# One scheduling block, ordered by a finer model, around the whole body of a two-block transformer kernel

## The chip, the cores and the metric

The kernel runs on one core of a Trainium2 chip. TensorE (PE) multiplies matrices, VectorE (DVE), ScalarE (ACT) and GpSimd (POOL) do the rest, and SyncE (SP) issues the DMA transfers. The metric is the time of one execution in microseconds (us). Each engine, and the queue on SP, works through its instructions in the order that the program gives it; the engines wait for each other on semaphores.

## The reference

Two transformer blocks follow each other on one sequence of 512 tokens of width 1024, all in fp32. The first has two layers that are modulated by a condition vector:

```python
cond = jax.nn.silu(c)
for layer in range(DEPTH):                       # DEPTH = 2
    mod = cond @ w_ada[layer] + b_ada[layer]     # 1024 -> 3 x 1024
    shift, scale, gate = jnp.split(mod, 3, axis=-1)
    h = rmsnorm(x, g_pre[layer]) * (1.0 + scale[:, None, :]) + shift[:, None, :]
    if layer % 2 == 0: y = even_mixer(h, ...)
    else:              y = odd_mixer(h, ...)
    x = x + gate[:, None, :] * rmsnorm(y, g_post[layer])
```

The even mixer has 8 heads of latent attention (MLA: low-rank queries, keys and values, plus a rotary part) and 8 heads of attention over a sliding window of 128 with sinks. The odd mixer has 4 heads of differential attention and 8 heads of forgetting attention. Each is gated by `silu` and multiplied by an output weight. The second block has one mixer with three parts: 6 heads of sparse attention (compressed, selected and windowed keys), 4 heads of stick-breaking attention, and 6 heads of HGRN, a gated recurrence worked out in chunks of 64 tokens; then the output weight, a scaled residual and a layer norm.

## The kernel before, in words

All tensors are held with the width or the tokens on the 128 partitions. The products keep fp32 accuracy by splitting each operand into a high and a low part (`hh`, `hl` of the activations; `whi`, `wlo` of the weights): one product is three matmuls (`mm3`, whose matmuls have line L79). A weight piece of 128 x 1024 comes by DMA into `wraw` (L106), ACT casts it to `whi` (L108) and DVE forms the residue `wlo` (L112); this loader has a raised priority (`WP`).

The stages run in this order: setup and the first h (0 to 60 us in the profile), projection and rotary steps (to 115), the sliding-window heads (to 211), the MLA setup (to 250) and MLA heads (to 309), the output product with the first residual (to 345), the odd mixer (to 610), the second residual (to 646), and the second block: projections and the HGRN scan (to about 803), stick-breaking (to 869), sparse attention (to 991), and the output product with the layer norm.

The modulation is worked out in the background. `gemv_steps` yields one step at a time: `wada` loads a 128 x 1024 piece of `w_ada` into the tile `graw` (L156), and `gemv_acc` adds it, times an element of `cond`, to the accumulator `sa` on DVE (L174 for the first of eight pieces, L176 for the others). `graw` has one buffer, so a piece can be loaded only when the product before it is done. Heads call `hook`, which takes steps of this background product and, by a credit, weight chunks from the queue `fq`, so that PE has filling beside the softmax work. In the program's names `sa_435` is the accumulator of the first layer's gate, and `sa_777` that of the second layer's gate.

The residual (L601 to L614) forms row statistics, adds the gated output to x, and then `hgen` (L238, L240) normalises each block of rows, which PE transposes into the new `hh` and `hl`. In the MLA setup the keys and queries of a pair of heads are split into four tiles (`qk_425` to `qk_428`, L326) and copied to other partitions by DMA (L366). In the HGRN scan the score products are `sr <- sa, tmpr`.

No order is written out by hand: the Tile framework's scheduler takes the instructions in the order in which the code makes them, with the priorities above, and decides how they stand on each engine and on SP's queue. The rotating buffers (PSUM: `acc` 3, `s` 2, `t` 2, `o` 1; SBUF: `wraw` 2, `whi` 4, `graw` 1 and others) are fixed in the tables at the head of the class `Kern`. The change touches the first line of `build`, which makes the whole body.

Of the kernel before, what the change touches and what calls it, by code (L numbers as in the profile page):

```python
# [1716 lines left out]


def build(tc, I, O, stage=3):
    with ExitStack() as ctx:  # L1720
        K = Kern(ctx, tc, I, O)
        nc = K.nc
        K.setup()
        K.modv = {}

        def done0(part, acc):
            K.mod_done(part, acc)

        def steps0():
            yield from K.gemv_steps(1, (0, 1), K.mod_done)  # L1730
            yield from K.gemv_steps(0, (2,), lambda part, acc: K.gate_sum(0, acc))

        K.back = steps0()
        og = K.even()
        K.bg(100)
        put = lambda b, xb: nc.sync.dma_start(O["out"][b * 128:(b + 1) * 128, :], xb)
        if stage == 1:
            K.residual(I["w_out0"], [2, 3, 0, 1], og, put)
            return
        a1 = K.mod_a(1, K.modv[1])  # L1740
        nc.vector.tensor_scalar(a1, a1, -0.5, None, ALU.mult)
        rows = K.spread(a1), K.spread(K.modv[0])
        K.new_h()
        xd = K.dram([4, 128, D])

        def nxt(b, xb):
            nc.sync.dma_start(xd[b], xb)
            return K.hgen(b, xb, rows)

        K.residual(I["w_out0"], [2, 3, 0, 1], og, nxt)  # L1750
        K.xd = [xd[b] for b in range(4)]
        K.back = K.gemv_steps(1, (2,), lambda part, acc: K.gate_sum(1, acc))
        og = K.odd()
        K.bg(100)
        if stage == 2:
            K.residual(I["w_out1"], [0, 1, 2, 3], og, put)
            return
        K.new_h()
        xd2 = K.dram([4, 128, D])

        def nxt2(b, xb):
            nc.sync.dma_start(xd2[b], xb)
            return K.hgen(b, xb)

        K.residual(I["w_out1"], [0, 1, 2, 3], og, nxt2)
        K.xd = [xd2[b] for b in range(4)]
        tr = K.load("cst_2", [128, 512], "cst")
        K.strict = tr[:, 256:384]
        K.ones2 = tr[:, 384:512]
        K.tri = K.t([128, 128], "tri", 1, F32R)  # L1770
        K.mones = K.t([128, 128], "mones", 1, F32R)
        nc.vector.tensor_copy(K.tri, tr[:, 0:128])
        nc.vector.tensor_copy(K.mones, tr[:, 128:256])
        og = K.second()
        K.tail(I["w_out2"], K.TO, og)
# [148 lines left out]
```

## Time and profile before

| | |
|---|---|
| median of 3 runs | 1039.86 us (1039.27 to 1048.97) |
| profiled execution | 1036.68 us, span 1035.0 us |
| mean granted TensorE clock | 0.974 of full speed |
| PE, DVE, ACT, POOL busy | 934.3, 709.4, 535.8, 246.2 us |
| DMA queue, share of 16 engines | 44.9% |

The span runs from the first to the last instruction of the profiled execution; its own time is 1.7 us longer. Busy time counts the time in which an engine has an instruction in work, so that idle time is the span less that. In the rows of the profile buffer numbers are left out of the names, and `L79` is line 79 of the kernel. A timeline row gives the start, the length, the engine, the line, the operation, output and inputs, and in brackets the idle time before and what ended it.

### The profile page before, as it was taken

What the parts mean: (1) busy time and instruction counts of PE and PEld (TensorE: products, weight loads), DVE (VectorE), ACT (ScalarE), POOL (GpSimd) and SP (SyncE); (2) the same over time, 40 slices, a digit from 0 to 9 for tenths busy, and PEclk for the clock granted to TensorE, in tenths of its full rate; (3) what the DMA queues carried; (4) which work ended last, traced back from release to release, by engine and by line L of the source; (5) the groups of instructions that cost most, each with busy time, mean ns of one, the idle gap of its engine ahead of it and who ended that gap; (6) DMA issues with size and microseconds to landing.
All of it is one profiled execution on the core that took longest, in us unless ns stands there. A gap on an engine that the chain in (4) does not pass through costs nothing.

```text
span 1035.0 us, 14792 instructions
## 1 busy us (share of the span) xinstructions
PE 934.3 (90%) x4999; PEld 766.3 (74%) x4999; DVE 709.4 (69%) x1581; ACT 535.8 (52%) x1181; POOL 246.2 (24%) x274
## 2 busy tenths in 40 slices
PE   3989996878998899999999999999977989999896
PEld 2767875766776887788887778987866768777675
DVE  5876665866877866875366666466689486577757
ACT  6433653836754434475355843454533484565820
POOL 1220122201430002221011420043145133444440
PEclk9899998889999999999999999999999999999998
DMA  9656544365556366661564343343401623331242
GB/s 359 221 170 200 147 100 134 90 148 137 168 169 199 121 209 166 158 168 42 164 152 117 133 138 121 100 123 107 138 21 52 170 51 97 103 95 38 64 140 82
DMA packets 56672, 137.38 MB, mean 133 GB/s; under 512 B 15048, under 2 KB 15432, under 8 KB 56597
## 3 DMA queue, kind: packets, MB, share of 16 engines
q1 hardware_dynamic: 56596, 136.44, 44.9%
q8 instruction: 40, 0.66, 0.3%
q14 instruction: 36, 0.29, 0.1%
HBM read 105.42 MB, written 8.44 MB: 110 GB/s over the span
## 4 chain that ended last, share of the span: by engine, by line
PE 39%; DVE 9%; ACT 4%; issue 2%; POOL 2%; DMA 1%; SPq 0%; DVEq 0%; POOLq 0%; ACTq 0%
PE accr L79 28%; PE sr L79 5%; PE o L79 3%; PE tr L139 2%; DVE ptl L94 1%; DVE hl L94 1%; DMA qk<-qk 1%; ACT whir L108 1%; ACT Pr L384 1%; DVE pthr L93 1%; POOL tmpr L1636 0%; DVE Pr L93 0%; DVE tmpr L1633 0%; DVE tmpr L1634 0%; DVE wlor L112 0%
## 5 line engine op out<-in xcount | busy, mean ns | idle before, releaser
L79 PE MATMUL accr<-hh,whir 128*128 128x512 f32 x516 | 207.2, 402 | 5.4 <-DVE V L94 4.7
L79 PE MATMUL accr<-hl,whir 128*128 128x512 f32 x516 | 206.5, 400 | 1.2 <-DVE hl L689 1.1
L79 PE MATMUL accr<-hh,wlor 128*128 128x512 f32 x516 | 204.3, 396 | 0.0
L108 ACT CAST whir<-wrawr 128x1024 fp32r<-128x1024 f32 (+5 forms) x110 | 111.4, 1014 | 119.1 <-PE accr L79 73.6
L112 DVE TENSOR_TENSOR wlor<-wrawr,whir 128x1024 fp32r<-128x1024 f32 (+6 forms) x93 | 113.1, 1219 | 68.7 <-ACT whir L108 68.2
L394 POOL TENSOR_SCALAR Pr<-Pr,sm 128x256 f32<-128x256 f32 (+2 forms) x120 | 74.7, 638 | 281.8 <-DVE sm L816 74.2
L79 PE MATMUL accr<-whir,hh 128*128 128x256 f32 (+4 forms) x364 | 119.2, 328 | 4.3 <-DVE V L94 1.9
L384 ACT ACTIVATE Pr<-Pr,nm 128x256 f32<-128x256 f32 (+3 forms) x176 | 95.6, 545 | 52.0 <-DVE nm L382 51.6
L79 PE MATMUL accr<-wlor,hh 128*128 128x256 f32 (+4 forms) x364 | 118.0, 324 | 2.5 <-DVE wlor L112 2.5
L79 PE MATMUL accr<-whir,hl 128*128 128x256 f32 (+4 forms) x364 | 119.1, 328 | 0.6 <-DVE hl L94 0.6
L79 PEld LDWEIGHTS accr<-hh,whir 128*128 128x128 f32 x516 | 98.5, 191 | 25.1 <-issue 5.8
L79 PEld LDWEIGHTS accr<-hl,whir 128*128 128x128 f32 x516 | 98.3, 191 | 20.8 <-DVE hl L689 2.1
L79 PEld LDWEIGHTS accr<-hh,wlor 128*128 128x128 f32 x516 | 98.2, 190 | 19.7 <-issue 0.4
L79 PE MATMUL sr<-qk,qk 128*128 128x256 f32 (+11 forms) x400 | 93.6, 338 | 9.5 <-DVE nm L382 5.3
L94 DVE TENSOR_TENSOR ptl<-tr,pthr 128x256 fp32r<-128x256 f32 (+3 forms) x160 | 71.2, 464 | 27.1 <-ACT pthr L89 24.0
L139 PE MATMUL tr<-ident,Pr 128*128 128x128 f32 x392 | 70.4, 288 | 18.4 <-DVE ptl L94 10.1
L79 PEld LDWEIGHTS sr<-qk,qk 128*128 128x128 f32 (+2 forms) x400 | 63.2, 192 | 24.7 <-DVE nm L382 13.0
L79 PEld LDWEIGHTS accr<-whir,hh 128*128 128x128 f32 x364 | 70.1, 193 | 10.7 <-issue 3.6
L79 PEld LDWEIGHTS accr<-wlor,hh 128*128 128x128 f32 x364 | 70.2, 193 | 7.2 <-DVE wlor L112 3.1
L89 ACT CAST pthr<-tr 128x384 fp32r<-128x384 f32 (+3 forms) x124 | 52.2, 440 | 44.2 <-PE tr L139 43.3
L139 PEld LDWEIGHTS tr<-ident,Pr 128*128 128x128 f32 x392 | 46.8, 146 | 37.0 <-issue 17.5
L79 PEld LDWEIGHTS accr<-whir,hl 128*128 128x128 f32 x364 | 69.8, 192 | 6.0 <-DVE hl L94 1.3
(370 smaller groups left out, 1725.4 us busy)
## 6 DMA issues: line engine op xcount, KB each, us to landing
graw<-in_w_ada_dram SPq DMA_DIRECT2D x32, 512.0 KB
wrawr<-in_w_od_dram SPq DMA_DIRECT2D x30, 512.0 KB
wrawr<-in_w_dram SPq DMA_DIRECT2D x29, 512.0 KB
qk<-qk SPq DMA_DIRECT2D x111, 128.0 KB
wrawr<-in_w_out_dram SPq DMA_DIRECT2D x24, 512.0 KB
wrawr<-in_w_ev_dram SPq DMA_DIRECT2D x17, 512.0 KB
V<-in_w_ada_dram SPq DMA_DIRECT2D x14, 512.0 KB
qk<-tmpr SPq DMA_DIRECT2D x34, 128.0 KB
```

What stands on the lines that cost most here:

```text
L79: self.nc.tensor.matmul(out, a, b, start=start, stop=stop, skip_group_check=True)
L89: self.nc.scalar.copy(hi, src)
L93: self.nc.vector.tensor_copy(hi, src)
L94: self.nc.vector.tensor_tensor(lo, src, hi.bitcast(F32), ALU.subtract)
L108: self.nc.scalar.copy(hi[:, :n], raw[:, :n])
L112: eng.tensor_tensor(lo[:, :n], raw[:, :n], hi[:, :n].bitcast(F32), ALU.subtract)
L139: self.nc.tensor.transpose(out, in_, self.ident[:k, :k])
L384: nc.scalar.activation(Pi, Pi, AF.Exp, bias=nm[:, i:i + 1], scale=-1.0, accum_out=s[:, i:i + 1])
L394: self.nc.gpsimd.tensor_scalar(v, v, r[:, i:i + 1], 1.0, ALU.mult, ALU.mult)
```

## The change

The body of `build` is put into one block of the Tile framework for which its scheduler uses a finer model of engines and queues:

```diff
@@ -1717,7 +1717,7 @@
 def build(tc, I, O, stage=3):
-    with ExitStack() as ctx:
+    with tc.block(schedule_with_timeline_sim=True), ExitStack() as ctx:
         K = Kern(ctx, tc, I, O)
         nc = K.nc
         K.setup()
```

Every engine keeps the instructions that it had (ACT has one table load less); what changes is the order on each engine and on SP's queue. Three places follow. The last number in a name is the scheduler's own and shifts by one.

In the MLA setup, the SP queue stood like this before; `graw` are the pieces of `w_ada`, `wrawr1_634` an output weight, and `qk_429<-qk_425` and so on the copies for the first pair of heads:

```order
L156 DMA graw_458_2171<-in_w_ada_dram 128x1024
L254 DMA d608_2808<-moda_607_2805 128x8x1
L208 DMA V_615_2819<-in_b_gate_dram 128x1024
L209 DMA V_615_2819<-in_g_post_dram 128x1024
L156 DMA graw_472_2230<-in_w_ada_dram 128x1024
L106 DMA wrawr1_634_2877<-in_w_out0_dram 128x1024
L366 DMA qk_429_2056<-qk_425_2052 64x512
L366 DMA qk_430_2057<-qk_426_2053 64x512
L366 DMA qk_431_2058<-qk_427_2054 64x512
L366 DMA qk_432_2059<-qk_428_2055 64x512
L366 DMA qk_425_2052<-hh_363_1741 32x512
```

and stands like this now:

```order
L156 DMA graw_458_2172<-in_w_ada_dram 128x1024
L254 DMA d608_2809<-moda_607_2806 128x8x1
L156 DMA graw_472_2231<-in_w_ada_dram 128x1024
L156 DMA graw_502_2350<-in_w_ada_dram 128x1024
L106 DMA wrawr1_634_2878<-in_w_out0_dram 128x1024
L156 DMA graw_518_2422<-in_w_ada_dram 128x1024
L366 DMA qk_429_2057<-qk_425_2053 64x512
L366 DMA qk_430_2058<-qk_426_2054 64x512
L366 DMA qk_431_2059<-qk_427_2055 64x512
L366 DMA qk_425_2053<-hh_363_1742 32x512
L366 DMA qk_432_2060<-qk_428_2056 64x512
```

Two more pieces of `w_ada` (502 and 518) stand ahead of the copies. On DVE the same place read as follows before, from the second piece's product to the first mask and maximum (L382) of a head:

```order
L176 SCALAR_TENSOR_TENSOR sa_435_2087<-graw_458_2171,cond_5_72,sa_435_2087 128x1024
L94 TENSOR_TENSOR V_414_1983<-accr2_418_2007,V_414_1983 128x4x64
L94 TENSOR_TENSOR V_414_1983<-accr0_419_2018,V_414_1983 128x4x64
L112 TENSOR_TENSOR wlor1_529_2462<-wrawr1_527_2460,whir1_528_2461 128x640
L94 TENSOR_TENSOR V_415_1984<-accr2_418_2007,V_415_1984 128x4x64
L94 TENSOR_TENSOR V_415_1984<-accr0_419_2018,V_415_1984 128x4x64
L326 TENSOR_TENSOR qk_426_2053<-accr1_423_2035,qk_425_2052 128x512
L176 SCALAR_TENSOR_TENSOR sa_435_2087<-graw_472_2230,cond_5_72,sa_435_2087 128x1024
L326 TENSOR_TENSOR qk_428_2055<-accr2_424_2045,qk_427_2054 128x512
L112 TENSOR_TENSOR wlor2_629_2841<-wrawr0_627_2839,whir2_628_2840 128x1024
L112 TENSOR_TENSOR wlor3_636_2879<-wrawr1_634_2877,whir3_635_2878 128x1024
L326 TENSOR_TENSOR qk_443_2115<-accr0_440_2097,qk_442_2114 128x512
```

and now, from the product with piece 472:

```order
L176 SCALAR_TENSOR_TENSOR sa_435_2088<-graw_472_2231,cond_5_73,sa_435_2088 128x1024
L94 TENSOR_TENSOR V_414_1984<-accr1_417_1997,V_414_1984 128x4x64
L94 TENSOR_TENSOR V_415_1985<-accr1_417_1997,V_415_1985 128x4x64
L94 TENSOR_TENSOR V_414_1984<-accr2_418_2008,V_414_1984 128x4x64
L112 TENSOR_TENSOR wlor1_529_2463<-wrawr1_527_2461,whir1_528_2462 128x640
L94 TENSOR_TENSOR V_415_1985<-accr2_418_2008,V_415_1985 128x4x64
L176 SCALAR_TENSOR_TENSOR sa_435_2088<-graw_502_2350,cond_5_73,sa_435_2088 128x1024
L326 TENSOR_TENSOR qk_426_2054<-accr1_423_2036,qk_425_2053 128x512
L176 SCALAR_TENSOR_TENSOR sa_435_2088<-graw_518_2422,cond_5_73,sa_435_2088 128x1024
L112 TENSOR_TENSOR wlor2_629_2842<-wrawr0_627_2840,whir2_628_2841 128x1024
L326 TENSOR_TENSOR qk_428_2056<-accr2_424_2046,qk_427_2055 128x512
```

The products with pieces 502 and 518 now stand ahead of the split `qk_428`; before they came among the heads' work.

At the start of the first residual DVE had this order before (L215 forms the gate row, L601 and L602 the row statistics and gated rows, L112 weight residues):

```order
L215 TENSOR_TENSOR V_615_2819<-o_617_2826,V_615_2819 128x512
L112 TENSOR_TENSOR og_667_3024<-wrawr1_666_3023,og_667_3024 128x1024
L601 TENSOR_SCALAR ss1_619_2831<-ss1_619_2831 128x1
L602 TENSOR_TENSOR V_618_2830<-accr0_623_2835,V_615_2819 128x512
L601 TENSOR_SCALAR ss1_620_2832<-ss1_620_2832 128x1
L602 TENSOR_TENSOR V_618_2830<-accr1_624_2836,V_615_2819 128x512
L601 TENSOR_SCALAR ss1_621_2833<-ss1_621_2833 128x1
L602 TENSOR_TENSOR V_618_2830<-accr2_625_2837,V_615_2819 128x512
L112 TENSOR_TENSOR V_665_3019<-wrawr0_664_3018,V_665_3019 128x1024
L601 TENSOR_SCALAR ss1_622_2834<-ss1_622_2834 128x1
L602 TENSOR_TENSOR V_618_2830<-sr0_626_2838,V_615_2819 128x512
L112 TENSOR_TENSOR wlor0_747_3348<-wrawr1_745_3346,whir0_746_3347 128x792
L174 TENSOR_SCALAR sa_777_3622<-graw_778_3623,cond_5_72 128x1024
```

and has this one now:

```order
L215 TENSOR_TENSOR V_615_2820<-o_617_2827,V_615_2820 128x512
L174 TENSOR_SCALAR sa_777_3623<-graw_778_3624,cond_5_73 128x1024
L112 TENSOR_TENSOR og_667_3025<-wrawr1_666_3024,og_667_3025 128x1024
L601 TENSOR_SCALAR ss1_619_2832<-ss1_619_2832 128x1
L602 TENSOR_TENSOR V_618_2831<-accr0_623_2836,V_615_2820 128x512
L176 SCALAR_TENSOR_TENSOR sa_777_3623<-graw_789_3677,cond_5_73,sa_777_3623 128x1024
L601 TENSOR_SCALAR ss1_620_2833<-ss1_620_2833 128x1
L602 TENSOR_TENSOR V_618_2831<-accr1_624_2837,V_615_2820 128x512
L601 TENSOR_SCALAR ss1_621_2834<-ss1_621_2834 128x1
L602 TENSOR_TENSOR V_618_2831<-accr2_625_2838,V_615_2820 128x512
L601 TENSOR_SCALAR ss1_622_2835<-ss1_622_2835 128x1
L602 TENSOR_TENSOR V_618_2831<-sr0_626_2839,V_615_2820 128x512
```

The product with piece 778 moved from behind the row statistics to their head, and the one with 789 into them; those with 798, 802, 813, 829, 833 and 836 follow in the residual, all but 836 ahead of the second L240.

In the HGRN scan PE had this order before, between two score products of the scan and the transposes behind them:

```order
L79 MATMUL sr0_1493_7271<-sa_1339_6457,tmpr1_1490_7250 128x128 x4
L79 MATMUL accr1_1541_7540<-wlor1_1538_7482,hh_1207_5841 128x256
L79 MATMUL accr1_1541_7540<-whir2_1537_7481,hl_1208_5842 128x256
L79 MATMUL accr1_1541_7540<-whir2_1537_7481,hh_1207_5841 128x256
L79 MATMUL accr1_1541_7540<-wlor1_1538_7482,hh_1207_5841 128x256
L79 MATMUL accr1_1541_7540<-whir2_1537_7481,hl_1208_5842 128x256
L79 MATMUL sr1_1495_7285<-sa_1339_6457,tmpr2_1492_7264 128x128 x4
L79 MATMUL sr0_1496_7292<-sa_1339_6457,tmpr3_1494_7278 128x128 x4
L79 MATMUL tr1_1505_7329<-V_1306_6287,tmpr2_1503_7325 128x128
L79 MATMUL tr0_1506_7333<-V_1306_6287,tmpr2_1503_7325 128x128
L79 MATMUL o_1498_7300<-graw_1479_7193,V_1306_6287 64x128 x8
L79 MATMUL tr1_1507_7337<-V_1306_6287,tmpr2_1503_7325 128x128
```

and has this one now, from the score product 1493 on:

```order
L79 MATMUL sr0_1493_7272<-sa_1339_6458,tmpr1_1490_7251 128x128 x4
L79 MATMUL accr1_1553_7640<-hh_1207_5842,wlor3_1552_7636 128x512
L79 MATMUL accr1_1553_7640<-hh_1207_5842,whir0_1551_7635 128x512
L79 MATMUL accr1_1553_7640<-hl_1208_5843,whir0_1551_7635 128x512
L79 MATMUL accr1_1553_7640<-hh_1207_5842,wlor3_1552_7636 128x512
L79 MATMUL accr1_1553_7640<-hh_1207_5842,whir0_1551_7635 128x512
L79 MATMUL accr1_1553_7640<-hl_1208_5843,whir0_1551_7635 128x512
L79 MATMUL sr1_1495_7286<-sa_1339_6458,tmpr2_1492_7265 128x128 x4
L79 MATMUL accr1_1553_7640<-hh_1207_5842,wlor3_1552_7636 128x512
L79 MATMUL accr1_1553_7640<-hh_1207_5842,whir0_1551_7635 128x512
L79 MATMUL accr1_1553_7640<-hl_1208_5843,whir0_1551_7635 128x512
L79 MATMUL accr1_1553_7640<-hh_1207_5842,wlor3_1552_7636 128x512
```

Where 1495 and 1496 followed each other, twelve matmuls of a weight chunk (`accr1_1553`, 512 wide) now lie between them; that chunk stood near the scan's end before.

## Rows read from the trace of the kernel before

**Rows 1.** The page, part 1 (engines) and part 4 (the chain, by engine).

```profile
PE 934.3 (90%) x4999; PEld 766.3 (74%) x4999; DVE 709.4 (69%) x1581; ACT 535.8 (52%) x1181; POOL 246.2 (24%) x274
PE 39%; DVE 9%; ACT 4%; issue 2%; POOL 2%; DMA 1%; SPq 0%; DVEq 0%; POOLq 0%; ACTq 0%
```

**Rows 2.** Windows by stage, with the columns in the first line.

```profile
core 0: us, PE busy (x) PEld busy (x) DVE busy (x) ACT busy (x) POOL busy (x), PEclk, DMA share, GB/s
211.00:250.00 39.00, 30.57 (x134) 23.24 (x133) 22.92 (x57) 16.10 (x40) 4.27 (x7) 0.91 0.71 157
309.00:345.00 36.00, 32.02 (x168) 26.66 (x167) 29.73 (x66) 17.42 (x47) 3.27 (x1) 1.00 0.60 194
```

**Rows 3.** Waits of PE: line waited for, total us, times, longest us.

```profile
PE accr L79 <- DVE V L94: 6.6, 2, 4.7
PE o L79 <- DVE pthr L176: 3.1, 1, 3.1
```

**Rows 4.** Timeline of the SP queue, start us first, then length us.

```profile
213.93 0.33 SPq L156 DMA_DIRECT2D graw<-in_w_ada_dram  x1
224.44 0.33 SPq L156 DMA_DIRECT2D graw<-in_w_ada_dram  x1
226.25 6.05 SPq L366 DMA_DIRECT2D qk<-qk  x4
...
363.73 0.33 SPq L156 DMA_DIRECT2D graw<-in_w_ada_dram  x1
```

**Rows 5.** Timeline of DVE, with idling before and its releaser in brackets.

```profile
213.16 0.74 DVE L174 TENSOR_SCALAR sa<-graw,cond 128x1024 f32<-128x1024 f32 x1
223.12 1.28 DVE L176 SCALAR_TENSOR_TENSOR sa<-graw,cond,sa 128x1024 f32<-128x1024 f32 x1 [4.59 <-DMA graw<-in_w_ada_dram]
229.93 1.28 DVE L176 SCALAR_TENSOR_TENSOR sa<-graw,cond,sa 128x1024 f32<-128x1024 f32 x1 [2.86 <-DMA graw<-in_w_ada_dram]
231.13 0.68 DVE L326 TENSOR_TENSOR qk<-accr,qk 128x512 fp32r<-128x512 f32 x1
...
367.59 1.28 DVE L176 SCALAR_TENSOR_TENSOR sa<-graw,cond,sa 128x1024 f32<-128x1024 f32 x1
```

**Rows 6.** Timeline of PE in the MLA setup.

```profile
226.28 0.77 PE L79 MATMUL accr<-hh,whir 128*128 128x512 f32 x1 [4.72 <-DVE V L94]
...
233.41 0.40 PE L79 MATMUL accr<-hl,whir 128*128 128x512 f32 x1
233.64 0.39 PE L79 MATMUL accr<-hh,wlor 128*128 128x512 f32 x1
...
239.19 0.40 PE L79 MATMUL sr<-qk,qk 96*128 96x128 f32 x2
```

**Rows 7.** Windows inside the MLA setup, columns as in rows 2.

```profile
221.50:226.50 5.00, 0.28 (x2) 0.24 (x2) 3.38 (x7) 1.19 (x3) 0.00 (x0) 0.73 0.82 134
226.50:232.00 5.50, 5.50 (x16) 4.36 (x17) 2.64 (x4) 1.53 (x2) 1.05 (x1) 0.63 0.84 253
```

**Rows 8.** Timeline of DVE in the first residual.

```profile
308.76 0.69 DVE L215 TENSOR_TENSOR V<-o,V 128x512 f32<-128x512 f32 x1 [1.20 <-PE o L79]
...
335.68 0.74 DVE L613 SCALAR_TENSOR_TENSOR Pr<-V,st_r,Pr 128x512 f32<-128x512 f32 x1
336.34 0.74 DVE L614 SCALAR_TENSOR_TENSOR Pr<-tmpr,st_r,Pr 128x512 f32<-128x512 f32 x1
...
338.21 1.40 DVE L238 SCALAR_TENSOR_TENSOR Pr<-Pr,st_r,pthr 128x512 f32<-128x512 f32 x2
339.53 1.28 DVE L240 TENSOR_TENSOR Pr<-Pr,pthr 128x512 f32<-128x512 f32 x2
```

**Rows 9.** Windows around the HGRN scan, columns as in rows 2.

```profile
745.00:803.00 58.00, 45.79 (x314) 38.23 (x313) 50.78 (x103) 22.02 (x41) 29.60 (x33) 0.97 0.14 40
803.00:833.00 30.00, 29.17 (x137) 23.32 (x136) 17.68 (x36) 17.31 (x37) 5.60 (x12) 1.00 0.59 147
```

**Rows 10.** The page, part 5: the DVE residue of a weight.

```profile
L112 DVE TENSOR_TENSOR wlor<-wrawr,whir 128x1024 fp32r<-128x1024 f32 (+6 forms) x93 | 113.1, 1219 | 68.7 <-ACT whir L108 68.2
```

## The prediction

> **What bounds the kernel now.** First the page: TensorE (PE) is busy 934.3 of 1035.0 us, VectorE (DVE) 709.4, and the chain that ended last runs over PE for 39% of the span, with DVE next [rows 1]. So 100.7 us of PE idling is all that another order of the same instructions could win back, and the question is in which stages it lies and what ends it there. The windows by stage [rows 2] put much of it into stages that wait for DVE: of the 39 us that prepare the MLA heads, PE works 30.57; of the 36 us of the first residual, 32.02, with DVE at 29.73. The waits [rows 3] name the releasers: PE's accumulators wait 6.6 us for VectorE's V splits, and one `o` product waits 3.1 us for a step released through L176, the background product of `cond` and `w_ada`. Last the timeline of the DMA queue and of DVE around the background product [rows 4, 5], because the new order moves just those instructions.
>
> Since every engine keeps its instructions, nothing is cheaper or dearer by itself. Everything below is about what stands ahead of what. The order of the changed program shows thousands of rows in other places, so "the change does nothing" is excluded.
>
> **1. The HGRN scan gets more filling: -15 us.** Between the first and the last of the scan's score products (744.9 to 803 us before) the new PE order holds 103 more matmuls 512 wide and 24 fewer 256 wide ones. A 512-wide matmul starts 0.23 us after the one before it when they follow each other (233.41 and 233.64, [rows 6]), and at half the width I take half, so 103 x 0.23 - 24 x 0.12 = 20.8 us of work move into a stretch where PE is idle 12.2 of 58 us, and where its busy time of 45.79 is padded: a lone matmul is recorded for 0.39 us though it holds the array for 0.23 [rows 9, 6]. Behind it PE is the bound (29.17 of 30 us, [rows 9]), so what leaves there shortens the end: 20.8 us at most. Against it, the scan is a DVE stage (50.78 of 58), and its DVE zone takes four more weight residues at 1.2 us, two evictions and a V split, about 7.5 us in all [rows 9, 10]. If DVE packs tightly, 50.78 + 7.5 = 58.3, so the stretch grows by 0.3; if DVE keeps its present share of 0.88, by 8.6. That gives -20.5 to -12.2. I take -15, nearer the second, as DVE there is in step with GpSimd and PE.
>
> **2. The MLA setup waits for four weight pieces in a row: +8.7 us.** The background product has one buffer, `graw`: each piece is issued on SP once the last product has read it, so one round is landing plus product. The rows show 224.44 to 229.93, 5.5 us, DVE idling for it, and 363.73 to 367.59, 3.9 us, without idling [rows 4, 5]; under the load of 214 to 223 us it was 9.2. With the product's 1.28 a round takes 5.2 to 6.8 us; I take 6.0. Before, two products stand ahead of the last split of pair 0 (`qk_428`), now four, with little DVE work between. The first product of the row ends at 213.9 (213.16 + 0.74). The first landing I put at 7.35, the middle of 5.5 and 9.2; three rounds more start the last product at 239.2; product, a residue (1.2) and the split (0.68) end at 242.4 [rows 5, 10]. PE's next accumulator waits for that split, and 24 matmuls (5.5 us) precede the first score, now at 247.9 instead of 239.19 [rows 6]: +8.7. Bounds: 5.5 and rounds of 5.2 give 243.7, +4.5; 9.2 and 6.8 give 252.2, +13. The same pieces stand on SP ahead of the copies of pair 0, which began at 226.25 [rows 4]; they can now start when the third product has ended, near 234.5. That is 8.3 us later than before, inside the 8.7, so they do not end last.
>
> **3. The first residual waits for six: +9.6 us.** The products of the next gate, before spread to 380 us, now begin right behind L215 (308.76 + 0.69, [rows 8]); the first ends at 310.2, and six more stand between the row statistics and the normalisations. With a landing of 4.7 and five rounds of 6.0 the sixth starts at 344.9 and ends at 346.2. Behind it stand L238 twice, L613, L614 and L240 twice, 1.40 + 0.74 + 0.74 + 1.28 = 4.2 us, so the second normalised row block is ready at 350.4, not 340.8 [rows 8]: +9.6. Rounds of 5.2 give +4.8, of 6.8 +14.4. What waits is the transposes of the new h on PE, and with them all of the odd mixer. The products that later stages no longer have to run free DVE where PE is the bound, which is worth nothing.
>
> **4. The rest: +1 us.** Weight chunks come earlier in the sliding-window, MLA, forgetting and sparse heads, whose last heads then have less cover; small loads come earlier in the first 60 us. The nearest rows are the 100.7 us of idling [rows 1] and single waits of 3 to 7 us [rows 3]: -8 to +10.
>
> **Sum.** -15 + 8.7 + 9.6 + 1 = +4.3. The profiled execution took 1036.7 us, so 1041 us; it lies 3.2 us under the median of the three runs, 1039.86, and against that median 1041 is +0.1%. About 1% (10.4 us) is what a measurement of this kernel can tell from no change, so the forecast is no change: chance 0.37.
>
> **A rule beside terms 2 and 3.** The rows show 3.9 to 9.2 us from issue to use for a piece of 512 KB [rows 4, 5]. The Trainium skill, in "DMA: Bandwidth & Descriptors", section "Anatomy of one DMA — SWDGE (gpsimd) path", fits 2.0 us plus bytes over 436 GB/s for the software path; as an estimate that is 3.2 us here. By it a round would take 4.5 us, terms 2 and 3 would shrink to about +0.1 and +0.6, and the sum would be 1023. The rows are all longer, so they decide.
>
> **Rivals.** *Faster, 1022 us, chance 0.31:* rounds run at their shortest and the scan's filling is worth its most: 4.5 + 4.8 - 20.5 - 3 = -14. For it speaks that the 3.9 us landing is a row, that DVE has other work in line between the products, and that PE behind the scan is full. Against it, in the MLA setup the DMA engines and DVE's idling already showed rounds of 6.8.
>
> *Slower, 1061 us, chance 0.25:* the rounds stretch to 8 us, since V's loads and the output weights share the queue with the pieces, as they did in the 9.2 us landing [rows 4, 5]. The MLA setup then loses 213.9 + 9.2 + 24 + 3.2 + 5.5 - 239.2 = 16.6, the residual 310.2 + 6.7 + 40 + 1.3 + 4.2 - 340.8 = 21.6; with -15 and +1 that is +24. It decides from rounds of about 6.8 us on, where the sum passes +13. Against it, the long landing is one of many, and came as several loads of 512 KB were issued together.
>
> *Slower by the clock, 1052 us, chance 0.07:* after PE's stall of 4.72 us the granted clock was 0.73, and 0.63 in the 5.5 us behind it [rows 6, 7], between the levels of 1.2 and 2.4 GHz. Longer stalls would leave the chunk ahead of the first score at 0.63 (5.5 us become 8.7) and the residual's work partly so, some 8 us: +11 on the sum. The Trainium skill's "TensorE: Matmul & The Clock Gate", section "Loop structure matters more than you think", has PE drop to the low clock where a loop waits for DMA; the rows agree. It has little weight because PE mostly waits again right behind.
>
> **Numbers.** Faster by over 1%: 0.31 and a little of the forecast's low end, 0.32. Slower by over 1%: 0.25 and 0.07, 0.32. Within: 0.36. The ends of the terms reach from -20.5 + 4.5 + 4.8 - 8 = -19 to -12.2 + 13 + 14.4 + 10 = +25; both at once are unlikely, and the rivals lie just inside: 1019 to 1062.
>
> **What would show it.** Step 1: in the window around the scan PE near 0.9 busy, and the stretch from the scan's last score to the end some 20 us shorter. Step 2: four L176 products between 214 and 245 us, each with idling released by `graw`, and the first MLA score near 248. Step 3: six between 310 and 348, and the odd mixer starting about 10 us later than before. It is wrong if rounds are other than 6 us, if PE has filling during them, or if the late heads, robbed of cover, idle by far more than 10 us.

## The result, and the profile after

| | before | after |
|---|---|---|
| median | 1042.82 us (4 runs, 1039.27 to 1048.97) | 1093.7 us (4 runs, 1087.1 to 1095.12) |
| profiled execution, its span | 1036.68, 1035.0 us | 1087.1, 1085.4 us |
| mean granted TensorE clock | 0.974 | 0.945 |

The kernel became slower: ratio 1.047, 95% interval 1.040 to 1.054. The forecast of 1041 us and its range were wrong. The page of after, part 1 (engines) and part 4 (the chain), against [rows 1]:

```profile
PE 957.5 (88%) x4999; PEld 787.9 (73%) x4999; DVE 711.5 (66%) x1581; ACT 534.6 (49%) x1180; POOL 240.4 (22%) x274
...
PE 53%; DVE 19%; DMA 11%; ACT 7%; issue 5%; POOL 2%; SPq 1%; DVEq 0%; POOLq 0%; ACTq 0%
```

The instructions are the same, yet PE is busy 23.2 us longer and idles 27.2 us longer (127.9 us where there were 100.7). So about half of the loss is waiting, and about half is the same matmuls taking longer. The granted clock fits the second half: by the clock records of the two traces PE worked at the lower of its two levels (1.2 and 2.4 GHz) for 39 us before and for 90 after. In the chain that ended last, DVE rose from 9 to 19% and DMA from 1 to 11%.

The two traces, cut where PE ends the same piece of work, show where the 50.4 us lie. To set aside PE work that has moved between stretches, each matmul is reckoned at 0.213 us per 512 columns plus 0.015, the 0.228 us from one 512-wide matmul to the next [rows 6]; what a stretch takes beyond that sum is called its **excess**. The gate row is formed in two halves of 512 columns; both traces are cut behind the second.

| stretch, up to | before, us | after, us | more | more excess |
|---|---|---|---|---|
| the last sliding-window head | 210.9 | 219.6 | 8.8 | 7.3 |
| the first MLA score (setup) | 29.4 | 37.2 | 7.8 | 9.2 |
| the gate row behind the last MLA head | 68.5 | 80.5 | 12.0 | 12.4 |
| the first differential head's product with V (output product, first residual, projections) | 136.7 | 146.4 | 9.7 | 8.8 |
| the gate row behind the last forgetting head | 164.5 | 177.1 | 12.5 | 7.9 |
| the scan's last score | 193.6 | 208.4 | 14.7 | -4.2 |
| the last sparse head | 187.3 | 176.1 | -11.2 | 2.1 |
| the end | 44.1 | 40.1 | -4.0 | 6.8 |

Up to the gate row behind the MLA heads both kernels do the same PE work (205 us); the excess is 103 before and 132 after. A stretch of one trace is good to some 4 us: in the run further down that moves the products alone, the sliding-window heads have the same PE work between their products as before, and 4.1 us more excess.

**The MLA setup**, DVE's timeline of after, against [rows 5]: the products with `graw`, and the split that PE waits for.

```profile
219.76 0.74 DVE L174 TENSOR_SCALAR sa<-graw,cond 128x1024 f32<-128x1024 f32 x1
...
225.67 1.28 DVE L176 SCALAR_TENSOR_TENSOR sa<-graw,cond,sa 128x1024 f32<-128x1024 f32 x1 [2.39 <-DMA graw<-in_w_ada_dram]
...
234.52 1.28 DVE L176 SCALAR_TENSOR_TENSOR sa<-graw,cond,sa 128x1024 f32<-128x1024 f32 x1 [6.04 <-DMA graw<-in_w_ada_dram]
...
239.59 1.29 DVE L176 SCALAR_TENSOR_TENSOR sa<-graw,cond,sa 128x1024 f32<-128x1024 f32 x1 [0.95 <-DMA graw<-in_w_ada_dram]
...
245.54 1.28 DVE L176 SCALAR_TENSOR_TENSOR sa<-graw,cond,sa 128x1024 f32<-128x1024 f32 x1 [4.06 <-DMA graw<-in_w_ada_dram]
246.74 1.22 DVE L112 TENSOR_TENSOR wlor<-wrawr,whir 128x1024 fp32r<-128x1024 f32 x1
247.88 0.68 DVE L326 TENSOR_TENSOR qk<-accr,qk 128x512 fp32r<-128x512 f32 x1
```

PE's timeline there, against [rows 6], and the windows, against [rows 2, 7]:

```profile
248.61 0.79 PE L79 MATMUL accr<-hh,whir 128*128 128x512 f32 x1 [5.43 <-DVE qk L326]
249.21 0.63 PE L79 MATMUL accr<-hl,whir 128*128 128x512 f32 x1
249.63 0.63 PE L79 MATMUL accr<-hh,wlor 128*128 128x512 f32 x1
...
253.53 0.39 PE L79 MATMUL accr<-hh,whir 128*128 128x512 f32 x1
253.76 0.39 PE L79 MATMUL accr<-hl,whir 128*128 128x512 f32 x1
...
256.26 0.85 PE L79 MATMUL sr<-qk,qk 96*128 96x128 f32 x6
```

```profile
219.60:256.80 37.20, 24.54 (x85) 18.74 (x85) 15.16 (x24) 8.39 (x16) 1.05 (x1) 0.78 0.48 119
...
242.00:249.00 7.00, 1.57 (x7) 1.01 (x6) 3.46 (x4) 2.17 (x4) 0.00 (x0) 0.80 0.51 139
249.00:256.80 7.80, 7.80 (x29) 6.27 (x29) 1.89 (x3) 0.59 (x1) 0.00 (x0) 0.74 0.49 115
```

From the first product's end to the last one's start 25.0 us pass, where the prediction had 25.3. Behind them come the residue, the split, and PE's accumulator after 5.43 us of idling. Then the clock shows: matmuls follow each other every 0.42 us (249.21 to 249.63), later every 0.23 (253.53 to 253.76). The 24 matmuls before the first score take 7.65 us, not 5.5.

**The first residual**, DVE's timeline, against [rows 8]:

```profile
337.31 0.69 DVE L215 TENSOR_TENSOR V<-o,V 128x512 f32<-128x512 f32 x1 [1.57 <-PE o L79]
337.91 0.74 DVE L174 TENSOR_SCALAR sa<-graw,cond 128x1024 f32<-128x1024 f32 x1
...
342.57 1.27 DVE L176 SCALAR_TENSOR_TENSOR sa<-graw,cond,sa 128x1024 f32<-128x1024 f32 x1
...
354.46 1.29 DVE L176 SCALAR_TENSOR_TENSOR sa<-graw,cond,sa 128x1024 f32<-128x1024 f32 x1 [1.39 <-DMA graw<-in_w_ada_dram]
...
373.27 1.28 DVE L176 SCALAR_TENSOR_TENSOR sa<-graw,cond,sa 128x1024 f32<-128x1024 f32 x1 [1.32 <-DMA graw<-in_w_ada_dram]
...
377.12 1.29 DVE L240 TENSOR_TENSOR Pr<-Pr,pthr 128x512 f32<-128x512 f32 x2
```

The second product starts 3.9 us behind the first one's end (338.65 to 342.57; the sum had 4.7), and five rounds to 373.27 take 6.14 us each. The second row block is normalised 41.1 us behind the gate row (337.3 to 378.4), before 32.1 (308.7 to 340.8): +9.0, where the sum had +9.6.

**The last MLA heads**, PE's timeline, with idling and its releaser in brackets, and the window, which ends with the first half of the gate row:

```profile
314.40 0.74 PE L139 MATMUL tr<-ident,Pr 128*128 128x128 f32 x5 [0.82 <-DVE ptl L94]
315.70 0.50 PE L79 MATMUL o<-pthr,V 128*128 128x512 f32 x1 [0.57 <-ACT pthr L89]
...
319.52 0.74 PE L139 MATMUL tr<-ident,Pr 128*128 128x128 f32 x5 [0.94 <-DVE ptl L94]
320.82 0.50 PE L79 MATMUL o<-pthr,V 128*128 128x512 f32 x1 [0.57 <-ACT pthr L89]
```

```profile
312.60:334.40 21.80, 15.58 (x67) 9.96 (x65) 9.44 (x19) 7.78 (x15) 2.55 (x2) 0.86 0.21 73
```

Here no engine is full: PE has 8.7 us of matmul work at 0.228 us per 512 columns, DVE is busy 9.44 us and ACT 7.78 of 21.8. Transposes, splits and products with V simply follow each other, and nothing else is left to put between them. Before, these three heads had part of the output product between them. From the fifth head's end to that of the whole gate row the excess is 15.5 us (312.6 to 337.3), before 5.4 (281.2 to 308.7).

PE's waits, first of before and then of after: what the new order waits for longer are splits and copies of the setup, the normalised rows of the residual and the maxima (`nm`) of the heads.

```profile
PE tr L139 <- DVE ptl L94: 10.1, 14, 2.1
...
PE sr L79 <- DVE nm L382: 5.3, 10, 1.2
...
PE sr L139 <- DVE Pr L240: 3.5, 2, 2.3
...
PE sr L79 <- DMA qk<-qk: 1.2, 2, 0.7
...
PE accr L79 <- DVE qk L326: 0.7, 1, 0.7
```

```profile
PE tr L139 <- DVE ptl L94: 11.0, 19, 4.1
...
PE sr L79 <- DVE nm L382: 9.0, 17, 1.7
PE sr L139 <- DVE Pr L240: 7.3, 3, 3.5
PE accr L79 <- DVE qk L326: 6.1, 2, 5.4
PE sr L79 <- DMA qk<-qk: 6.0, 3, 5.1
```

**The scan and what follows**, windows between the same pieces of work, of before and then of after (columns as in rows 2):

```profile
745.50:803.60 58.10, 45.89 (x314) 38.29 (x314) 50.32 (x101) 22.02 (x41) 29.60 (x33) 0.97 0.13 37
803.60:832.70 29.10, 28.27 (x135) 22.73 (x134) 17.38 (x36) 17.04 (x36) 5.30 (x12) 1.00 0.60 148
```

```profile
795.10:869.20 74.10, 65.99 (x401) 55.47 (x399) 55.74 (x111) 27.91 (x53) 29.55 (x33) 0.95 0.30 79
869.20:900.70 31.50, 29.55 (x168) 25.73 (x167) 18.92 (x45) 19.47 (x42) 10.68 (x15) 0.95 0.49 127
```

The scan has 21.5 us more matmul work (53.6 for 32.1) in 16.0 us more (74.1 for 58.1): 5.5 us of excess won. What becomes of them behind it is the next question.

### The profile page after: what moved, and what is told of

It reads as the page before. It is cut to its first block, busy times and chain, and to the rows that moved or that the text cites. A ratio compares the mean times of both kernels' runs of the same rounds, so it can differ in the third digit from the quotient of the medians.

```text
span 1085.4 us, 14853 instructions
## 1 busy us (share of the span) xinstructions
PE 957.5 (88%) x4999; PEld 787.9 (73%) x4999; DVE 711.5 (66%) x1581; ACT 534.6 (49%) x1180; POOL 240.4 (22%) x274
## 4 chain that ended last, share of the span: by engine, by line
PE 53%; DVE 19%; DMA 11%; ACT 7%; issue 5%; POOL 2%; SPq 1%; DVEq 0%; POOLq 0%; ACTq 0%
PE accr L79 38%; PE sr L79 7%; PE o L79 5%; DMA graw<-in_w_ada_dram 5%; PE tr L139 2%; DVE wlor L112 2%; DMA qk<-qk 2%; DVE sa L176 2%; DMA wrawr<-in_w_out_dram 2%; DVE ptl L94 1%; DVE Pr L382 1%; SPq L366 1%; ACT whir L108 1%; POOL wlor L112 1%; DMA tmpr<-tmpr 1%
## 5 line engine op out<-in xcount | busy, mean ns | idle before, releaser
L112 DVE TENSOR_TENSOR wlor<-wrawr,whir 128x1024 fp32r<-128x1024 f32 (+6 forms) x93 | 115.8, 1248 | 74.7 <-ACT whir L108 74.4
L79 PE MATMUL accr<-whir,hh 128*128 128x256 f32 (+4 forms) x364 | 122.0, 338 | 12.2 <-ACT hh L89 5.0
L394 POOL TENSOR_SCALAR Pr<-Pr,sm 128x256 f32<-128x256 f32 (+2 forms) x120 | 71.7, 615 | 275.3 <-DVE sm L1153 72.7
L79 PE MATMUL accr<-wlor,hh 128*128 128x256 f32 (+4 forms) x364 | 120.8, 332 | 0.3 <-DVE wlor L112 0.3
L79 PEld LDWEIGHTS accr<-hh,wlor 128*128 128x128 f32 x516 | 98.6, 191 | 21.9 <-POOL wlor L112 2.1
L139 PE MATMUL tr<-ident,Pr 128*128 128x128 f32 x392 | 74.9, 297 | 14.0 <-DVE ptl L94 10.8
L79 PEld LDWEIGHTS sr<-qk,qk 128*128 128x128 f32 (+2 forms) x400 | 65.4, 195 | 29.6 <-DVE nm L382 15.9
L79 PE MATMUL o<-pthr,V 128*128 128x512 f32 (+1 forms) x192 | 59.2, 329 | 9.5 <-ACT pthr L89 5.0
```

The source lines that it names most:

```text
L79: self.nc.tensor.matmul(out, a, b, start=start, stop=stop, skip_group_check=True)
L112: eng.tensor_tensor(lo[:, :n], raw[:, :n], hi[:, :n].bitcast(F32), ALU.subtract)
L139: self.nc.tensor.transpose(out, in_, self.ident[:k, :k])
L394: self.nc.gpsimd.tensor_scalar(v, v, r[:, i:i + 1], 1.0, ALU.mult, ALU.mult)
```

## The experiments

The theory after the result: **G**, PE filling (chunks, projections, output product, scores) that the new order runs as soon as it is ready leaves the later heads bare (without PE work beside their softmax), and a low granted clock adds to each wait; beside it the two rows of background products cost as forecast. Rivals: the products carry nearly all, or the heads are bound by DVE and ACT and do not care. Ratios are to the kernel before, run on the same chip. The runs with a table below write the new order into the kernel before without any block, and one of them has 4.1 of the 4.7%; so it is the order that costs, and hardly the block as such.

**Parts of the changed kernel held back.** Background products:

```diff
+            with self.tc.issue_after(self.last("vector")):     # gemv_acc, L174, L176
```

> The changed kernel, with each background product (L174, L176) queued behind the DVE instruction that the code makes just before it, so that the finer model can't bring it forward; all else free. Theory A (the products' wait for their pieces costs what the MLA setup and the first residual lost, 9.3 + 11.7 us more time without matmul work than before): about 1073 us, the first MLA score some 9 us earlier after the sliding-window heads and the odd mixer earlier by about 21 in all. Theory B (the loss is the cover taken from the late heads; the products only fill idle DVE time): 1088 to 1095, no change. If both hold a part: between.

Measured: 1089.01 us, ratio 1.0455 (1.0406 to 1.0505), theory B's range. The excess of the MLA setup fell from 20.0 to 6.5 us, but that of the sliding-window heads and the MLA heads rose (that of the second and third MLA head from 2.7 to 9.9). No product stands in the first residual any more (the first one is at 389 us), yet the excess up to the residual's last transposes is still 16.7 us; the change had 19.9, before 11.0.

```diff
+            with self.tc.issue_after(self.last("tensor")):     # fill() and trickle(): the chunks
```

> The changed kernel, with the matmuls of every weight chunk that the heads take as filling queued behind the PE instruction that the code makes just before the chunk; the products are free as in the change. Theory B (chunks used up early leave the last heads of each stage without cover: 6.6 us in the sliding-window heads, 9.3 in the MLA heads, 3.3 in the forgetting heads, 8 in sparse attention and tail): about 1066 to 1070. Theory A: no change, 1088 to 1095, since the products stand where the change put them.

> The changed kernel with both holds, products and chunks. A and B together: 1043 to 1050, the kernel before within 1%, and the scan may still be 5 us better. A alone: 1073. B alone: 1068. If it stays over 1060 after both, something else of the new order (transfers on the SP queue, the order of splits and residues) carries the loss.

Measured: the chunks held 1143.33 us, ratio 1.0963 (1.0904 to 1.1022), and both together 1131.68 us, 1.0858 (1.0794 to 1.0921). Neither brought the cover back; the waits for `nm` rose to 22 us with the chunks held. Both are far slower than any range expected. That tells nothing of the chunks in the change: a hold on one part of an order made by a planner is a new order.

**The products alone, in the kernel before:**

```diff
+            if pr == 0:
+                self.bg(4)
+                with self.tc.issue_after(self.last("vector")):
+                    self.half_split(ta[2], ta[3], pk)
...
+            self.bg(self.EB)           # first residual: one product ahead of each L602 and its twin
```

> The kernel before, its scheduler unchanged, with only the background products moved: the four pieces of the first gate ahead of the last split of the first MLA pair, and the eight of the second gate into the first residual, each ahead of a step of it. Theory A: +18 to +22 us, about 1062 to 1065, with first MLA score and odd mixer late by about 9 and 20. Theory B: 1040 to 1047.

Measured: 1062.0 us, ratio 1.0183 (1.0136 to 1.023), +18.6 us. The excess of the MLA setup rises from 10.7 to 16.8 us, that up to the last transposes of the first residual from 11.0 to 17.6. Its waits:

```profile
PE sr L139 <- DVE Pr L240: 9.9, 3, 6.3
...
PE accr L79 <- DVE V L94: 7.5, 2, 4.8
```

So moving the products alone costs what terms 2 and 3 of the prediction add up to (18.3 us), and it is not all of the loss. That the two waits alone make the 18.6 is not shown: this trace is 25.6 us longer than that of before, of which 6.1 lie in the setup, 6.6 up to the residual's last transposes and 7.4 in the MLA heads.

**The new order by stages**, written as a table into the kernel before:

```diff
+ORDER = {"PE": "170 7 7 7 -20 ...", "DVE": "...", ...}   # instruction numbers, as differences
+        reorder(tc)                                      # each behind the one ahead of it in the table
```

> The new order word for word on PE, and on DVE, ACT, POOL and SP but for the background products: each of the 32 products stands behind the DVE instruction that it followed before, and its load is placed by the scheduler as its buffer comes free. Theory A (the waits of the products are what the new order lost in the MLA setup and the first residual): 1070 to 1076 us, some 20 under the changed kernel, with the first MLA score some 9 us earlier after the sliding-window heads, and the odd mixer 20. Theory B (the loss is cover taken from the late heads and chains of evictions): 1085 to 1095.

> The kernel before, with each engine's new order for the instructions of the setup, the even mixer and the first residual alone; all later ones as the scheduler placed them before. By the tables of time without matmul work the new order lost about 26 us up to the last MLA head and some of the 12 behind it: 1072 to 1080 us. If the losses of the stages are not their own but passed on from one to the next: under 1060.

> The kernel before, with each engine's new order for the odd mixer and the second residual alone. By the tables: 5 to 14 us lost, 1048 to 1057. If the odd mixer lost only what the even one handed on: 1040 to 1047.

> The kernel before, with each engine's new order for the second block alone (scan, stick-breaking, sparse attention, tail). By the tables its filling of the scan gains 5.5 us and its later heads and tail lose 8 to 11, so 1042 to 1050: the term of -15 in the prediction is given back. If the scan's filling is a gain that only the loss ahead of it hid: 1025 to 1035.

| new order in | median, us | ratio (interval) |
|---|---|---|
| all but the background products | 1086.19 | 1.0414 (1.0374 to 1.0455) |
| even mixer and first residual | 1085.39 | 1.0421 (1.0382 to 1.0459) |
| odd mixer and its products | 1069.0 | 1.0264 (1.023 to 1.0298) |
| second block | 1040.14 | 0.9986 (0.9959 to 1.0014) |

The first lies in theory B's range. The even and the odd run are 5 and 12 us slower than the ranges expected, the second block is 2 us faster. The loss lies in the two mixers of the first block. In the odd run 13 us of excess come from the gate row to the first differential head (8 of them in the residual, into which its products move), 14 in its own heads and 4 behind them. The parts do not add up (4.2 + 2.6 - 0.1 = 6.7%, the change 4.7%), partly since the residual is in both runs. Putting the products back took the ratio from 1.047 to 1.041, some 6 us and not 18.6, and the intervals overlap; the setup's excess fell from 20.0 to 9.4 us, that up to the residual's last transposes only from 19.9 to 16.2, and that of the last two sliding-window heads and the column sums behind them rose from 11.7 to 17.6.

In the run with the second block alone the scan and the next stage look like this, as in the change:

```profile
746.80:821.30 74.50, 66.60 (x400) 56.36 (x399) 55.39 (x110) 27.66 (x52) 29.32 (x33) 0.95 0.30 78
821.30:854.00 32.70, 30.36 (x169) 25.62 (x168) 18.89 (x44) 20.73 (x42) 10.64 (x15) 0.95 0.48 124
```

The scan's excess falls by 4.7 us and that of the last three stick-breaking heads by 4.0; the first stick-breaking head (+3.5), the sparse heads (+3.0) and the output product (+5.5) give it back. Each of these is about as large as the scatter of one trace; the total of this run is what counts.

**PE's order alone, and scores held:**

```diff
+            with self.tc.issue_after(self.pv) if self.pv is not None else ExitStack():   # softmax, L380
                 smm(i, ps[:, :N])
```

> The kernel before, with a table that puts PE's instructions into the new order from the first to the last; the 32 background products stay on DVE where they stood before, and DVE, ACT, POOL and SP are otherwise ordered by the old scheduler around that. Theory P: the loss that is left when the products are put back lies in PE's order (work run ahead, late heads bare), so this kernel is as slow as the one with all engines in the new order and the products back: 1080 to 1090 us. Rival Q: PE's order only follows; the loss comes from where DVE, ACT and SP put residues, casts and loads, and with these back where they were it is 1043 to 1060 us.

> The changed kernel, with each head's score products on PE put behind the latest head's products with V that the code had made before them; this brings the PE work between the MLA heads' last products back to 3.6, 5.7, 7.8, 7.8, 5.7, 10.6, 1.7, 0.5 us (the change 7.5, 11.9, 3.6, 8.0, 1.9, 3.7, 2.7, 0.5; before 3.4, 4.7, 7.4, 6.4, 7.5, 6.1, 5.1, 3.0). Theory P: the score products that ran ahead took the cover from the last heads; the MLA heads' time beyond their matmul work falls from 27.8 to about 18 us, and the total by about 10: 1084 us, 1078 to 1088. Rival R: the MLA heads are bound by what DVE and ACT do for each head, and PE waits the same elsewhere: 1090 to 1096 us.

> The changed kernel with both: score products as in the run above, and the background products on DVE where the code makes them. Alone, the held products won 13.5 us in the MLA setup and lost most of it again in the heads (9.9 and 9.1 us beyond matmul work where the change had 2.7 and 8.8). Theory P: what was lost again was lost because scores ran ahead; held, the setup's 13 and the heads' 10 both stay: 1070 us, 1064 to 1078. Rival R: the heads are bound elsewhere and take the gain again: 1083 to 1092 us.

Measured: 1139.32 us (1.0924, 1.0873 to 1.0974), 1101.78 us (1.0562, 1.051 to 1.0614) and 1093.6 us (1.0473, 1.0422 to 1.0524). All three missed their theory; the third is 1.6 us above its rival's range, and its interval reaches into it. PE's new order, with the background products on DVE at their old places and the other engines ordered around it, is slower than both kernels, so it only says that the orders of the engines belong together. With the scores held, the last five MLA heads up to the gate row's first half have 34.0 us of work for 20.4, and an excess of 15.1 for 21.9; but the stretches around them lose more, and holding the products too brings the total back to that of the change, no further. What scores that run ahead cost by themselves, these holds can't tell; the run with early scores below tells more. Where the wait went, with both held:

```profile
PE sr L79 <- DVE nm L385: 11.2, 14, 1.8
PE o L79 <- ACT pthr L89: 10.9, 13, 1.9
PE tr L139 <- DVE ptl L94: 9.5, 18, 2.2
```

**A version that might beat both:** the table for the second block, but only for what the code makes ahead of the sparse attention.

> The kernel before, with only those instructions of the second block in the new order that its code makes ahead of the sparse attention. The scan keeps the new filling (24 us more matmul work up to the first stick-breaking head's end), but the work that it takes comes from several later heads (21.9, 20.7, 21.0 us of PE work up to the three points where there were 27.8, 36.5, 22.2), and the last sparse heads and the output product keep theirs (38.2 and 35.4, before 39.3 and 35.4). Theory S: the whole second block's new order gave nothing because the 5 us won in the scan were given back in the output product, which had 10.7 us less to do in parallel; kept, the end is 4 to 8 us earlier than before, 1034 to 1038. Rival T: what leaves a later stage leaves its waits as long as they were, and nothing is won: 1040 to 1045 us.

Measured: 1044.28 us, ratio 0.9998 (0.9972 to 1.0025), the rival's. The scan's 5 us stay won; the excess of the last three stick-breaking heads grows from 8.9 to 13.2 us and that of the sparse heads from 25.7 to 30.0, each about as large as the scatter of one trace.

**Single parts of the new order, by the code of the kernel before.** These make no holds on a finished order.

```diff
-    R = {'swa': 0.75, ...}
+    R = {'swa': 1.0, ...}
```

> The kernel before, with the credit for weight chunks in the sliding-window heads at 1.0 a head in place of 0.75, so that the code makes the chunks earlier: the PE work up to the first of these heads' products with V is 94.1 us (before 89.5), up to the fourth head's 7.7 (4.5; the change 14.7), and what lies between the last of them falls (8.0, 4.2, 3.8, 3.2, 2.5, 1.9 where there were 10.9, 7.7, 3.9, 2.2, 3.8, 2.5). Theory G: the filling is worth its time only where a head waits; taken early it leaves the later heads bare, and the end comes 3 to 9 us later: 1046 to 1052 us. Rival N: the heads waited for DVE and ACT anyway, and which of them has the chunks is the same: 1040 to 1044 us.

```diff
+                    with self.tc.issue_after(self.pvs[-2]) if i == 0 and not wide and len(self.pvs) == 8 else ExitStack():
                         self.mm3(acc[b], ...)      # outproj; pvs: the MLA heads' last products with V
```

> The kernel before, with the first half of the first output product held on PE until the seventh MLA head's product with V is done: 12 us of PE work leave the last four MLA heads (PE work between their products with V 3.6, 4.5, 2.3, 3.0, 6.0, 4.1 us where there were 7.4, 6.4, 7.5, 6.1, 5.1, 3.0; the change has 3.6, 8.0, 1.9, 3.7, 2.7, 0.5) and stand behind them, in front of the first residual. Theory G: the heads take as long without it, so the 12 us come on top, less what the residual hides: 8 to 12 us, 1051 to 1056 us. Rival N: the residual has 4 us of idling to take it in, and the heads run faster without it on PE: 1041 to 1047 us.

```diff
+            with self.tc.high_priority(offset=300 if self.phase == 'mla' else 0):
                 smm(i, ps[:, :N])
```

> The kernel before, with the score products of the MLA heads at a raised priority, so that they run ahead of other PE work as in the change, though less far (PE work between the products with V 4.2, 5.1, 8.9, 6.4, 5.5, 5.5, 4.5, 2.1 us). Theory G: run-ahead costs only where it leaves a head bare; here the work is spread as before, so the time stays within 4 us: 1040 to 1046 us. Rival R: scores that are done early hold buffers and put DVE's and ACT's work in the wrong turn: 8 us or more, from 1050 us on.

> The kernel before with three parts of the new order by hand, all else in the old: the background products early (alone 1062.0 us, ratio 1.018), the sliding-window chunks early, and the first half of the output product late. Theory G: these are the parts of the change that cost, each in its place, so the sum is 18.6 plus about 5 plus about 10: 1072 to 1082 us, near the 1085 of the kernel that has the new order in the even mixer and first residual alone. Rival N: the waits of the products take in the rest, since PE idles there anyway and the moved work fills it: 1060 to 1068 us, and most of the even mixer's 43 us lies elsewhere.

| part | median, us | ratio (interval) | more, us |
|---|---|---|---|
| chunks earlier | 1048.3 | 1.0062 (1.0039 to 1.0085) | 6 |
| output product late | 1050.26 | 1.008 (1.0047 to 1.0113) | 8 |
| scores early | 1046.59 | 1.0029 (0.9998 to 1.0059) | 4, not told from none |
| products, chunks and output product | 1071.69 | 1.028 (1.0236 to 1.0325) | 29 |

The first lies in G's range, the others within one microsecond of theirs; all lie 3 to 4 us outside the rivals'. What bare heads cost is seen in the last three MLA heads and the gate row, here in the run with the output product late; of before the same stretch is shown first (columns as in rows 2):

```profile
281.20:308.70 27.50, 25.64 (x131) 19.50 (x130) 20.86 (x41) 15.78 (x34) 7.66 (x8) 1.00 0.61 206
```

```profile
280.70:309.50 28.80, 23.38 (x102) 17.81 (x101) 23.88 (x44) 17.61 (x36) 8.93 (x8) 0.82 0.56 170
```

There are 29 matmuls fewer (6.3 us), and the stretch takes 1.3 us more: the heads run at their own pace, and PE's granted clock falls from 1.00 to 0.82. The three parts, 18.6 + 6 + 8 = 33 us one by one, make 29 together. In the run with all three the setup window reads much like that of the change:

```profile
220.40:256.70 36.30, 24.16 (x91) 18.38 (x91) 15.90 (x26) 9.66 (x18) 1.04 (x1) 0.80 0.76 160
```

## Why the prediction was wrong

**Terms 2 and 3 came out at their size.** The rounds were 5.1 to 8.9 us in the setup and 6.14 us in the residual (forecast 6.0). Setup: the first score came 35.8 us behind the first product's end, forecast 34.0, before 25.3: +10.5 for +8.7; the rest is the low clock. Residual: the second row block +9.0 for +9.6. The products moved alone cost 18.6 us, forecast 18.3. The setup's mechanism is borne out, since its excess is back at 9.4 us, or below, where the products are put back or held (before 10.7). That of the residual is borne out only in part: without its products, or with them at their old places, its excess in the new order stays at 16.7 and 16.2 us (before 11.0, the change 19.9). So some 5 of the 9 us there have another cause, which is not shown, and the size of term 3 is partly luck. By the Trainium skill's fit ("DMA: Bandwidth & Descriptors", "Anatomy of one DMA — SWDGE (gpsimd) path") a round would, as an estimate, have been 4.5 us; no round in the changed kernel was that short, so the measurement decides.

**Term 1 was mis-sized.** The scan did take the filling, but won 5.5 us of excess for the 15 forecast, and what left the later stages had been cover of their heads, whose excess rose. The new order of the second block alone is worth nothing that can be measured. The step that failed is "behind it PE is the bound, so what leaves there shortens the end", read from 29.17 of 30 us in one window [rows 9]. That window holds the first stick-breaking head; the other three, the sparse heads and the output product lie behind it.

**Term 4 is the step that failed most: "+1 us", bounds -8 to +10.** Of the 50.4 us, 9.2 of excess lie in the setup and 8.8 from the gate row to the first differential head, near terms 2 and 3, and 4.7 in the second block. The other 28 stand in stretches that the sum passed over: 7.3 us up to the last sliding-window head, 12.4 in the MLA heads and 7.9 in the odd mixer's heads. The text named the cause ("whose last heads then have less cover") and gave it no working. Its bounds came from idling that the old order had, but the waits that a new order makes have no row in the trace of the old one. Its own last sign of being wrong, late heads that idle by far more than 10 us, came true in excess: the last three MLA heads and the last four forgetting heads, each with the gate row behind them, have 28.9 us of excess for 12.1 (15.5 for 5.4, and 13.4 for 6.7). Chunks early and the output product late are shown to cost 6 and 8 us.

**The clock had the wrong place.** The prediction began with "nothing is cheaper or dearer by itself" and took the 100.7 us of idling for all that an order can change; but the same matmuls kept PE busy 23.2 us longer. As a rival at 7 chances in 100 the clock was to cost +11 behind two stalls. In fact it was also low in stretches with many small gaps: 0.86 in the bare MLA heads, 0.82 in the same heads of the run with the output product late, beside 0.78 in the setup. Between PE's first and last matmul the excess grew by 49.2 us, of which 26.0 are idling between matmuls and 23.2 are matmuls beyond their full-clock spacing, gaps inside the pipeline included. The clock can account for all of the 23.2: of the 51 us that PE worked more at the lower level, half, 26 us, would be saved at the upper one; this is an estimate, no run separates it.

**The slower rival** (1061 us by rounds of 8 us) had the sign and not the mechanism: rounds were not longer.

**Still open.** The even mixer and first residual in the new order cost 43 us; 29 are shown part by part. Where the other 14 lie is seen in part: the two profiled executions are 8.0 us apart, and 6.8 of that stand between the gate row and the first differential head (excess 27.4 us in the new order, 20.6 with the three parts by hand). The cause is not shown. In the odd mixer no single part was moved: of the 14 us in its own heads in the odd run, the bare last four forgetting heads and the gate row hold half (13.6 for 6.7, in the change 13.4), which is a likely part, not tested. What the finer model takes for a transfer or a matmul, and why it runs ready work first, was not looked into.

## What to carry to other kernels

A scheduler that fills every hole at once can spend in the first heads what the last heads of a loop need; before a new order is priced, count PE's work between the heads' last products in both orders, and price each head that has lost its cover at its own dependent chain. Give the low clock of a stretch with gaps its own term, since here the matmuls took longer by nearly as much as the gaps grew. Test a planner's order by moving one part in the old kernel, not by holding one part of the new.

## What the runs showed that was not expected

Taking 6.3 us of matmuls out of three heads and the gate row behind them made the stretch 1.3 us longer, at a granted clock of 0.82 for 1.00. PE's new order with the other engines ordered around it cost 9.2%, twice the whole change. And after a wait of 5.43 us the matmuls followed each other at 0.42 us for four microseconds before they were back at 0.23, that is near the lower of the two clock levels (1.2 and 2.4 GHz) and then at the upper.
